# Strassen's product for the input projection of a pooling and memory-attention layer, two blocks of tokens at a time

## The chip, the core and the metric

The kernel runs on one core of a Trainium2 chip. The metric is the device time of one execution in microseconds (us); the kernel before has a median of 645.53 us over three runs (643.67 to 647.44). Work is issued to five engines that run side by side and wait for one another through semaphores: TensorE (PE, matrix products), VectorE (DVE), ScalarE (ACT), GpSimd (POOL) and SyncE (SP, here only an issuer of DMAs). Each engine takes its instructions strictly in order.

## The reference, cut to what matters

With one layer (DEPTH = 1) only the pooling mixer is used. S = 2048 tokens of width 1024, all in float32:

```
hn   = rms_norm(x, norm_g)                          # 2048 x 1024
proj = hn @ pool_w_in                               # 1024 -> 768 | 256 | 1024
u, mq, gate = split(proj)
tok  = ((causal window means of u, widths 2 4 8 16) - u) @ w_group * pool_scale
mem_o = softmax(mq @ mem_k.T / 8) @ mem_v           # 4 heads of 64, 256 memory rows
h    = x + (concat(tok, mem_o) * silu(gate)) @ w_out
out  = rms_norm(h, final_norm_g)
```

`mem_k` and `mem_v` come from the memory `mem` (256 rows) by its own norm and product `w_mem_kv`.

## The kernel before

Every product of float32 matrices is three products in float32r: each operand is split in a rounded part `hi` and a remainder `lo = src - hi` (`_split`, line 43), and `_mm3` (line 54) adds hi*hi, hi*lo and lo*hi. The split costs one cast and one subtraction per operand tile.

At the start the group weights and the scale are folded into the input weights of the mixer (lines 91 to 131: `wus`, the fold, result stored to DRAM as `w_z`). Then four blocks of 512 tokens follow (`block`, line 283). A block has its normalised tokens feature-major in `xh`, `xl` (`prep_block`). Its input projection is sixteen tiles of 128 output columns in the list `order`: two of memory queries ("q"), eight of gate ("g"), six of the pooled mixer ("z"). `project` does one: a 512 KB weight tile is loaded (`load_w`) into the pool `raw` (four buffers), split, and 8 x 3 products of 128 x 128 x 512 are accumulated in one PSUM bank. Scores, transposes and value products of the memory attention are written between the tiles of the same block. The result of every tile stays on chip: the gate in `sg`, the window sums in `win`, the product of both, split, in `bh`, `bl`.

The output projection follows: two halves of 512 columns (`dh`), for each four weight pieces of two 128-row tiles (`w_out[c, dh]`), each 4 token tiles x 2 x 3 products; then residual, sum of squares, last norm, store. The tokens of the next block are loaded and split while it runs (`prep_block` between the two halves; row statistics are gathered earlier by `load_rows` during the input projection).

In block 0 the tokens are not scaled by their row norm ahead of the product: `prep_block(0, None)` uses x * gain alone and the row scale is multiplied into the first results afterwards (`scale`). So the first block's products need neither the row statistics nor the memory.

The order of instructions on each engine is not the order in which they are written: the framework places them by a timeline of its own, except where `keep_in_program_order` or `issue_after` holds them. SP's DMAs of block 0 go in the order written (`_InOrder`).

Of the kernel before, what the change touches and what calls it, by code (L numbers as in the profile page):

```python
# [15 lines left out]
P = 128  # L16
D = 1024
S = 2048
KT = D // P            # 128-row tiles of d_model
BT = 512               # tokens per block  # L20
NB = S // BT
QT = BT // P           # token tiles per block
NMEM = 256
GD = 192               # channels per pooling group
NJ = 6                 # 128-channel tiles of the pooled mixer
WINDOWS = (2, 4, 8, 16)
HALO = 16
EPS = 1e-6


class _InOrder:
    """The queue of SP; until it is free, its transfers go in the order in which they are written down."""

    def __init__(self, tc):
        self.tc = tc
        self.free = False

    def dma_start(self, **kw):
        i = self.tc.nc.sync.dma_start(**kw)  # L39
        return i if self.free else self.tc.keep_in_program_order(i)  # L40


def _split(nc, hi, lo, src, hi_eng):
    """hi = src rounded to float32r, lo = src - hi (exact in float32r)."""
    if hi_eng == "pool":
        nc.gpsimd.tensor_scalar(hi, src, 1.0, 1.0, ALU.mult, ALU.mult)  # L46
    elif hi_eng == "act":
        nc.scalar.copy(hi, src)
    else:
        nc.vector.tensor_copy(hi, src)  # L50
    return nc.vector.tensor_tensor(out=lo, in0=src, in1=hi.bitcast(F32), op=ALU.subtract)  # L51


def _mm3(nc, ps, ahi, alo, bhi, blo, start, stop):
    """ps += a.T @ b from float32r halves of a and b."""
    nc.tensor.matmul(ps, lhsT=ahi, rhs=bhi, start=start, stop=False)  # L56
    nc.tensor.matmul(ps, lhsT=ahi, rhs=blo, start=False, stop=False)  # L57
    nc.tensor.matmul(ps, lhsT=alo, rhs=bhi, start=False, stop=stop)  # L58
# [3 lines left out]
def trunk(ctx, tc, x, xT, mem, memT, norm_g, mem_norm_g, w_mem, w_out, w_in, w_uT, w_g, p_scale, final_g,  # L62
          cinv, out):
    nc = tc.nc
    sp = _InOrder(tc)
    pool = lambda name, bufs, **kw: ctx.enter_context(tc.tile_pool(name=name, bufs=bufs, **kw))
    const = pool("const", 1)
    raw = pool("raw", 4)
    whl = pool("whl", 3)
    big = pool("big", 1)  # L70
    hp = pool("hp", 8)
    zp = pool("zp", 2)
# [8 lines left out]
    # products of zeros bring the tensor engine to its full clock while the first loads are under way  # L81
# [7 lines left out]
    spare = [big.tile([P, KT, BT], F32, name=n).rearrange("p k t -> p (k t)") for n in ("bh", "bl")]  # L89
    wus = [spare[k // 5][:, (k % 5) * 6 * P:(k % 5 + 1) * 6 * P].rearrange("p (g d) -> p g d", g=6) for k in range(KT)]  # L90
    wga = spare[1][:, 18 * P:24 * P].rearrange("p (g e) -> p g e", g=4)
    psc = spare[1][:, 24 * P:30 * P]
    wgb = zp.tile([P, BT], F32, name="rbc", bufs=1)[:, :2 * GD].rearrange("p (a e) -> p a e", a=2)
# [10 lines left out]
    # the last 64 rows of two groups stand on the two halves of the partitions, their columns side by side  # L104
    tails = [whl.tile([P, 2, 2, GD], F32R, name=n) for n in ("whi", "wlo")]
    for t in tails:
        nc.vector.memset(t.bitcast(F32), 0.0)
# [5 lines left out]
    for k in range(KT):  # L113
        zs = wus[k].rearrange("p g d -> p (g d)")
        ut = att.tile([P, 2, 2, P], F32R, name=("qh", "ql", "pth", "ptl")[k % 4], bufs=1)
# [8 lines left out]
        for a, ps in enumerate(pss):  # L124
            c = slice(2 * a * GD, 2 * (a + 1) * GD)
            if k < 6:
                nc.vector.tensor_tensor(out=zs[:, c], in0=ps.rearrange("p l e -> p (l e)"), in1=psc[:, c], op=ALU.mult)
            else:
                nc.scalar.copy(zs[:, c], ps.rearrange("p l e -> p (l e)"))
                nc.gpsimd.tensor_tensor(out=zs[:, c], in0=zs[:, c], in1=psc[:, c], op=ALU.mult)  # L130

# [4 lines left out]
    nc.scalar.dma_start(out=gx, in_=norm_g)  # L136
    half = const.tile([P, QT], F32, name="half")
    nc.vector.memset(half, -0.5)
    halo = const.tile([P, NJ, HALO], F32, name="halo")
    nc.vector.memset(halo, 0.0)  # L140

# [7 lines left out]
    def sum_sq(src, acc):  # L149
        n = src.shape[-1]  # L150
        junk = (small.tile([P, BT], BF16, name="junk", bufs=1)[:, :n] if n <= BT else
                att.tile([P, D], BF16, name="qh", bufs=1))
        nc.scalar.activation(out=junk, in_=src, func=AF.Square, accum_out=acc)  # L153

    def bcast_cols(r, n, dst):
        """dst[:, 128 t + i] = r[i, t] on every partition."""
        ps = ps_mm.tile([P, BT], F32, name="mm")
        for t in range(n):
            rb = small.tile([P, P], F32, name="rb", bufs=4)
            nc.vector.tensor_copy(rb, r[:, t:t + 1].broadcast_to([P, P]))  # L160
            nc.tensor.matmul(ps[:, t * P:(t + 1) * P], lhsT=rb, rhs=ident, start=True, stop=True)
        nc.vector.tensor_copy(dst, ps[:, :n * P])

# [1 line left out]
    # per head the same 64 rows of keys stand on both halves of the partitions  # L165
    khi = const.tile([P, 2, 2, NMEM], F32R, name="khi")
    klo = const.tile([P, 2, 2, NMEM], F32R, name="klo")
    # [tile of keys, pair of heads, head]: the even head's values as [high | low], the odd one's as [low | high]
# [415 lines left out]
```

## Time and profile before

| | us |
|---|---|
| median of three runs | 645.53 |
| span of the profiled execution, first to last instruction | 639.9 |
| PE busy | 613.8 |
| DVE busy | 448.2 |
| POOL busy | 257.5 |
| ACT busy | 236.1 |
| bytes moved by DMA | 93.60 MB |

The page gives the span of the profiled execution; the time of that execution as the runs count it is not listed beside it. The median is 5.6 us above the span, and that difference is used wherever a span is turned into a time. A busy PE is not PE at its peak: products overlap, so that the duration of one (392 ns) is longer than the distance between two.

### The profile page before, as it was taken

To read this page: it belongs to the slowest core of one execution; us is meant where nothing else is said; L and a number is where in the kernel's file an instruction comes from. 1 tells how busy PE (TensorE), PEld (TensorE's weight loads), DVE (VectorE), ACT (ScalarE), POOL (GpSimd) and SP (SyncE) were. 2 spreads that over 40 slices of the span, in tenths; PEclk is the share of its full clock that TensorE was granted. 3 is DMA by queue.
4 is the path that set the end of the run, shared out by engine and by line. 5 is a ranking of instruction groups with operands and counts; after the bars stand their busy time and mean duration, and the time that the engine had idled before them with its cause. 6 is when DMAs were issued, how large, how long until landed. Compare 5 with 4: busy or idle time off the path is not lost.

```text
span 639.9 us, 8205 instructions
## 1 busy us (share of the span) xinstructions
PE 613.8 (96%) x2939; PEld 512.4 (80%) x2939; DVE 448.2 (70%) x673; ACT 236.1 (37%) x503; POOL 257.5 (40%) x211
## 2 busy tenths in 40 slices
PE   7999998999699999999899999999899999999995
PEld 5979786887588888888688888888688888888884
DVE  4875799999938279885847478885846558887235
ACT  2723255533113375522212475522211354532002
POOL 3623384332214155552224155553324254453243
PEclk9999997999999999999999999999899999999998
DMA  8979933413536933232546953232545722132103
GB/s 277 401 232 314 314 139 98 100 66 83 176 128 233 285 44 123 82 99 66 184 145 222 304 43 111 94 99 66 164 135 179 244 69 67 66 99 99 66 1 132
DMA packets 36841, 93.60 MB, mean 146 GB/s; under 512 B 5568, under 2 KB 13120, under 8 KB 36800
## 3 DMA queue, kind: packets, MB, share of 16 engines
q1 hardware_dynamic: 34288, 86.25, 43.9%
q10 hardware_dynamic: 2512, 6.82, 2.9%
q8 instruction: 23, 0.38, 0.2%
q14 instruction: 18, 0.15, 0.1%
HBM read 76.80 MB, written 11.54 MB: 138 GB/s over the span
## 4 chain that ended last, share of the span: by engine, by line
PE 56%; DVE 18%; DMA 10%; issue 5%; POOL 4%; ACT 4%; SPq 1%; ACTq 0%; POOLq 0%; DVEq 0%
PE mm L57 17%; PE mm L58 17%; PE mm L56 17%; DVE wlo L51 5%; DMA raw<-in_xT 3%; POOL win L350 2%; DVE win L364 2%; DMA raw<-w_z 2%; DVE raw L275 2%; PE mm L413 1%; SPq L39 1%; DVE pr L390 1%; DMA h<-in_xT 1%; PE pt L401 1%; DMA raw<-in_w_in 1%
## 5 line engine op out<-in xcount | busy, mean ns | idle before, releaser
L46 POOL TENSOR_SCALAR whi<-raw 128x1024 fp32r<-128x1024 f32 x100 | 127.4, 1274 | 284.8 <-PE mm L57 135.0
L58 PE MATMUL mm<-xh,wlo 128*128 128x512 f32 x512 | 200.7, 392 | 1.7 <-DVE wlo L51 1.7
L56 PE MATMUL mm<-xh,whi 128*128 128x512 f32 x512 | 200.7, 392 | 0.0
L57 PE MATMUL mm<-xl,whi 128*128 128x512 f32 x512 | 200.5, 392 | 0.0
L51 DVE TENSOR_TENSOR wlo<-raw,whi 128x1024 fp32r<-128x1024 f32 x100 | 134.2, 1343 | 57.5 <-POOL whi L46 57.5
L58 PEld LDWEIGHTS mm<-xh,wlo 128*128 128x128 f32 x512 | 96.5, 189 | 22.7 <-DVE wlo L51 2.9
L56 PEld LDWEIGHTS mm<-xh,whi 128*128 128x128 f32 x512 | 96.7, 189 | 18.7
L57 PEld LDWEIGHTS mm<-xl,whi 128*128 128x128 f32 x512 | 96.5, 189 | 18.6 <-DVE xl L272 0.3
L57 PE MATMUL mm<-wlo,bh 128*128 128x512 f32 x248 | 98.2, 396 | 5.7 <-DVE wlo L51 5.7
L56 PE MATMUL mm<-whi,bh 128*128 128x512 f32 x248 | 95.0, 394 | 4.9 <-DVE h L515 4.9
L58 PE MATMUL mm<-whi,bl 128*128 128x512 f32 x248 | 97.1, 394 | 0.0
L350 POOL TENSOR_TENSOR win<-win 128x525 f32<-128x525 f32 (+4 forms) x40 | 62.7, 1567 | 3.1
L153 ACT ACTIVATE junk<-h 128x512 bf16<-128x512 f32 (+1 forms) x33 | 20.4, 618 | 116.9 <-DVE h L515 116.8
L57 PEld LDWEIGHTS mm<-wlo,bh 128*128 128x128 f32 x248 | 47.4, 191 | 16.7 <-DVE wlo L51 6.9
L56 PEld LDWEIGHTS mm<-whi,bh 128*128 128x128 f32 x248 | 47.2, 190 | 15.5 <-issue 5.3
L58 PEld LDWEIGHTS mm<-whi,bl 128*128 128x128 f32 x248 | 47.3, 191 | 9.8
L350 POOL TENSOR_TENSOR win<-z 128x527 f32<-128x527 f32 x24 | 29.6, 1235 | 25.2 <-DVE z L337 10.7
L385 ACT ACTIVATE pr<-sc,nm 128x256 f32<-128x256 f32 x64 | 29.7, 470 | 18.4 <-DVE nm L381 18.2
L390 DVE TENSOR_SCALAR pr<-pr,rc 128x256 f32<-128x256 f32 x64 | 34.3, 577 | 0.9
L364 DVE SCALAR_TENSOR_TENSOR win<-win,z 128x512 f32<-128x512 f32 (+1 forms) x32 | 30.4, 949 | 4.2 <-POOL win L350 3.7
L515 DVE TENSOR_TENSOR h<-mm,h 128x512 f32<-128x512 f32 x31 | 21.1, 686 | 16.8 <-PE mm L58 16.7
L335 ACT COPY z<-halo 128x16 f32<-128x16 f32 x24 | 4.8, 203 | 73.9 <-DVE win L364 53.0
(157 smaller groups left out, 771.8 us busy)
## 6 DMA issues: line engine op xcount, KB each, us to landing
raw<-in_w_in SPq DMA_DIRECT2D x40, 512.0 KB, 4.5
raw<-in_w_out SPq DMA_DIRECT2D x32, 512.0 KB, 3.4
raw<-w_z SPq DMA_DIRECT2D x24, 512.0 KB, 4.6
h<-in_x SPq DMA_DIRECT2D x16, 512.0 KB, 6.8
raw<-in_xT SPq DMA_DIRECT2D x12, 512.0 KB, 4.1
out_y<-h ACTq DMA_DIRECT2D x12, 512.0 KB, 2.9
mq<-win SPq DMA_DIRECT2D x32, 128.0 KB, 6.0
h<-in_xT SPq DMA_DIRECT2D x4, 512.0 KB, 8.9
```

Source lines behind the costliest of these rows:

```text
L46: nc.gpsimd.tensor_scalar(hi, src, 1.0, 1.0, ALU.mult, ALU.mult)
L51: return nc.vector.tensor_tensor(out=lo, in0=src, in1=hi.bitcast(F32), op=ALU.subtract)
L56: nc.tensor.matmul(ps, lhsT=ahi, rhs=bhi, start=start, stop=False)
L57: nc.tensor.matmul(ps, lhsT=ahi, rhs=blo, start=False, stop=False)
L58: nc.tensor.matmul(ps, lhsT=alo, rhs=bhi, start=False, stop=stop)
L153: nc.scalar.activation(out=junk, in_=src, func=AF.Square, accum_out=acc)
L275: nc.vector.scalar_tensor_tensor(out=xk, in0=xk, scalar=g, in1=rb, op0=ALU.mult, op1=ALU.mult)
L350: nc.gpsimd.tensor_tensor(out=cur[rows, a:], in0=prev[rows, a:], in1=prev[rows, off:N - step], op=ALU.add)
L364: nc.vector.scalar_tensor_tensor(out=yt[rr], in0=sums[g][rr, HALO:], scalar=1.0 / WINDOWS[g], in1=z[rr, HALO:], op0=ALU.mult, op1=ALU.subt ...
L385: nc.scalar.activation(out=pr[:, h, :], in_=ps[:, h, :], func=AF.Exp, bias=nm[:, h:h + 1], accum_out=su[:, h:h + 1])
L390: nc.vector.tensor_scalar_mul(pr[:, h, :], pr[:, h, :], rc[:, h:h + 1])
L515: added = nc.vector.tensor_tensor(out=h, in0=ps, in1=h, op=ALU.add)
```

## The change

The input projection is done for two blocks (1024 tokens) and two column tiles at a time, by Strassen's product in the form with seven products (Winograd's): the depth of 1024 is cut in two halves, the two blocks are the two columns of B, the two weight tiles the two rows of A. `group` forms four sums of weight quarters on POOL and makes seven products of depth 512 (4 x 3 matmuls each); `x_forms` makes the seven token operands, which fill fourteen slots. Query, gate and pooled results go through DRAM (`q_d`, `g_d`, `y_d`) and are read back for the attention and for `branch` in the output projection; half of the second pair's token operands go through DRAM too (`xs_d`). The attention of both blocks is written between the products. The scale of the rows is in the tokens from the start. Pools: `raw` has three buffers instead of four, and carries rows, tokens, weights and branch tiles alike; the row tiles kept in `hp` and the double weight tiles in `whl` are gone.

```diff
@@ token operands @@
+    def x_forms(s, k, rbs, X, later):
+        r = []
+        for kk in (k, k + KH):
+            rt = raw_tile((P, 2, BT))
+            sp.dma_start(out=rt, in_=xT[2 * s:2 * s + 2, :, kk, :].rearrange("b p t -> p b t"))
+            for a in range(2):
+                nc.vector.scalar_tensor_tensor(out=rt[:, a, :], in0=rt[:, a, :], scalar=gx[:, kk:kk + 1], in1=rbs[a], ...)
+            r.append(rt)
+        b11, b12, b21, b22 = r[0][:, 0, :], r[0][:, 1, :], r[1][:, 0, :], r[1][:, 1, :]
+        t1, t2, t4 = (st.tile([P, BT], F32, name="s") for _ in range(3))
+        forms = {1: b11, 2: b21, 3: b22, 4: t4, 5: t1, 6: t2, 7: b12}
+        sub(g, t1, b12, b11)
+        sub(g, t2, b22, t1)
+        sub(g, b12, b22, b12)
+        sub(g, t4, b21, t2)
+        for p in (1, 6, 2, 5, 7, 3, 4):
+            if p in X:
+                _split(nc, X[p][0][:, k, :], X[p][1][:, k, :], forms[p], "act")
+        for i, p in enumerate(later):
+            nc.gpsimd.dma_start(out=xs_d[i, k], in_=forms[p])
@@ seven products for two column tiles @@
+    def group(s, X, w1, w2, take, between):
+        r1, r2 = raw_tile((P, KT, P)), raw_tile((P, KT, P))
+        sp.dma_start(out=r1, in_=w1)
+        sp.dma_start(out=r2, in_=w2)
+        a11, a12, a21, a22 = r1[:, :KH], r1[:, KH:], r2[:, :KH], r2[:, KH:]
+        add(g, s1, a21, a22)
+        sub(g, s2, s1, a11)
+        sub(g, a21, a11, a21)
+        sub(g, s4, a12, s2)
+        def product(p, onto=None):
+            hi, lo = chunk(forms[p], "act", (P, KH, P), "pool" if p in (2, 5, 3) else "dve")
+            ps = bank[p] = bank[onto] if onto else ps_mm.tile([P, BT], F32, name="mm")
+            for k in range(KH):
+                _mm3(nc, ps, hi[:, k, :], lo[:, k, :], X[p][0][:, k, :], X[p][1][:, k, :], ...)
+            between()
+            return ps
...
@@ output projection: operands read back @@
+    def branch(b, e, bh, bl):
+        rt = raw_tile((P, 2, BT))
+        sp.dma_start(out=rt[:, 0, :], in_=y_d[b][e])
+        sp.dma_start(out=rt[:, 1, :], in_=g_d[b][e])
+        nc.vector.tensor_tensor(out=rt[:, 0, :], in0=rt[:, 0, :], in1=rt[:, 1, :], op=ALU.mult)
+        _split(nc, bh[e // KH][:, e % KH, :], bl[e // KH][:, e % KH, :], rt[:, 0, :], "act")
...
-            for group in ((3,), (2,), (1, 0)):
-                ws = {c: load_w(w_out[c, dh], [P, 2, BT]) for c in group}
+            for ic, c in enumerate(order):
+                if dh == 0:
+                    for e in (2 * c, 2 * c + 1):
+                        branch(b, e, bh, bl)
+                wr = raw_tile((P, 2, BT))
+                sp.dma_start(out=wr, in_=w_out[c, dh])
+                ws = [chunk(wr[:, kk, :], "pool") for kk in range(2)]
+                between()
...
@@ the order of the whole @@
+    memory()
+    rbs = row_scales(0, row_stats(0))
+    for k in range(KH):
+        x_forms(0, k, rbs, X, ())
+    project_in(0, X, scales)          # scales: row statistics of blocks 2 and 3, between groups 7 and 8
+    project_out(0, (5, 7), ORDER, gf, some)   # some: x_forms(1, k) per weight piece
+    project_out(1, (3, 4), ORDER, gf, some)   # some: operands 5 and 7 read back
+    project_in(1, X, lambda: None)
+    project_out(2, (5, 7), ORDER, gf, lambda: None)
+    project_out(3, (3, 4), ORDER, gf, lambda: None)
```

PE's queue before, from the last products of the fold (`ptl` and `bl` hold input weights, `whi` group weights) to the first products of the input projection (`xh`, `xl`: tokens of block 0):

```order
L121 MATMUL mm<-bl 128x192 x2
L56 MATMUL mm<-whi,ptl 128x384
L57 MATMUL mm<-wlo,ptl 128x384
L58 MATMUL mm<-whi,ptl 128x384
L56 MATMUL mm<-xh,whi 128x512
L57 MATMUL mm<-xl,whi 128x512
L58 MATMUL mm<-xh,wlo 128x512
```

PE's queue of the change where its first product of the input projection stands (`x5h` and `wh` above it are the memory and its weights, `rb` the row statistics of the memory and of both blocks, `x1h` the token operand of product 1):

```order
L53 MATMUL sc<-x5h,wl 128x256 x2
L52 MATMUL pt<-wl,x5h 128x256
L53 MATMUL pt<-wh,x5l 128x256
L171 MATMUL mm<-ident,rb 128x128 x10
L51 MATMUL mm<-x1h,wh 128x512
L52 MATMUL mm<-x1l,wh 128x512
L53 MATMUL mm<-x1h,wl 128x512
```

The first products of the input projection have moved from behind the fold to behind the memory's products and the row statistics of two blocks.

SP's queue before, from the loads of the fold to the products of the memory (`h` is the pool `hp`):

```order
L39 DMA bl<-in_w_uT 128x768 x3
L39 DMA raw<-in_w_in 128x1024
L39 DMA h<-in_xT 128x1024 x4
L39 DMA raw<-in_w_in 128x1024 x2
L39 DMA h<-in_x 128x1024 x4
L39 DMA raw<-in_w_in 128x1024
L39 DMA gm<-in_mem_norm_g 128x8
L39 DMA raw<-in_memT 128x1024 x2
L39 DMA raw<-in_w_mem 128x1024 x2
```

The same queue of the change, from the memory's weights to the first weight tiles of the input projection:

```order
L196 DMA raw<-in_w_mem 128x1024 x2
L583 DMA w_z<-x4l 128x6x128 x2
L162 DMA raw<-in_mem 128x1024 x2
L162 DMA raw<-in_x 128x1024 x8
L272 DMA raw<-in_xT 128x2x512 x8
L306 DMA raw<-in_w_in 128x1024
L307 DMA raw<-in_w_in 128x1024
```

Rows, tokens and the first weight tiles now go one behind the other through the three buffers of `raw`, where before the tokens came first and had buffers of their own.

SP's queue before in the output projection of block 1 (blocks 2 and 3 alike):

```order
L39 DMA raw_2709<-in_w_out 128x1024
L39 DMA raw_2739<-in_w_out 128x1024
L39 DMA raw_2769<-in_w_out 128x1024
L39 DMA raw_2775<-in_w_out 128x1024
L39 DMA raw_2831<-in_xT 128x1024
L39 DMA raw_2839<-in_xT 128x1024
```

The same queue of the change in the first half of the output projection of block 0, one weight piece and the start of the next (`y_d0` and `g_d0` are the results read back):

```order
L500 DMA raw_2681<-y_d0_287 128x512
L501 DMA raw_2681<-g_d0_291 128x512
L553 DMA raw_2687<-in_w_out 128x1024
L272 DMA raw_2697<-in_xT 128x2x512
L272 DMA raw_2701<-in_xT 128x2x512
L500 DMA raw_2746<-y_d0_287 128x512
L501 DMA raw_2746<-g_d0_291 128x512
L500 DMA raw_2752<-y_d0_287 128x512
L501 DMA raw_2752<-g_d0_291 128x512
L553 DMA raw_2758<-in_w_out 128x1024
```

Each weight piece of this half now stands with two branch tiles and two token tiles in the same three buffers.

## Rows read from the trace of the kernel before

**Rows 1.** The page's head and first part: span; busy time, share and instructions by engine.

```profile
span 639.9 us, 8205 instructions
PE 613.8 (96%) x2939; PEld 512.4 (80%) x2939; DVE 448.2 (70%) x673; ACT 236.1 (37%) x503; POOL 257.5 (40%) x211
```

**Rows 2.** Busy time by stretch: start:end, length, engines' busy us, granted clock, DMA.

```profile
280.00:320.00 40.00, 37.79 (x171) 31.14 (x170) 30.57 (x39) 9.49 (x20) 14.29 (x9) 1.00 0.40 127
320.00:440.00 120.00, 120.00 (x576) 100.37 (x575) 82.40 (x123) 50.35 (x109) 52.09 (x42) 1.00 0.50 140
440.00:480.00 40.00, 37.14 (x157) 30.26 (x156) 25.53 (x34) 8.95 (x19) 10.19 (x7) 0.96 0.43 133
```

**Rows 3.** Timeline of PE: start us, us, instruction; 27 products lie from one start to the next.

```profile
26.59 0.39 PE L56 MATMUL mm<-xh,whi 128*128 128x512 f32 x1
...
198.73 0.39 PE L56 MATMUL mm<-xh,whi 128*128 128x512 f32 x1
...
204.85 0.39 PE L56 MATMUL mm<-xh,whi 128*128 128x512 f32 x1
```

**Rows 4.** Groups of instructions by line, PE, first 110 us: count, busy us, mean ns.

```profile
L56 PE MATMUL mm<-xh,whi 128*128 128x512 f32 x84 | 33.7, 401 | 0.0
...
L58 PE MATMUL mm<-xh,wlo 128*128 128x512 f32 x83 | 33.3, 401 | 1.7 <-DVE wlo L51 1.7
```

**Rows 5.** DMA issues of the whole span: KB each, median us from issue to landing.

```profile
raw<-in_w_out SPq DMA_DIRECT2D x32, 512.0 KB, 3.4
h<-in_x SPq DMA_DIRECT2D x16, 512.0 KB, 6.8
raw<-in_xT SPq DMA_DIRECT2D x12, 512.0 KB, 4.1
```

**Rows 6.** Groups of instructions by line, whole span, shapes apart: count, busy us, mean ns.

```profile
L350 POOL TENSOR_TENSOR win<-z 128x527 f32<-128x527 f32 x24 | 29.6, 1235 | 25.2 <-DVE z L337 10.7 <-ACT z L339 6.5 <-ACT bh L48 6.1
L153 ACT ACTIVATE qh<-h 128x1024 bf16<-128x1024 f32 x16 | 16.9, 1056 | 20.3 <-DMA h<-in_x 20.0
L275 DVE SCALAR_TENSOR_TENSOR raw<-raw,gx,rbc 128x512 f32<-128x512 f32 x24 | 17.5, 778 | 17.5 <-DMA raw<-in_xT 13.7 <-issue 3.8
L51 DVE TENSOR_TENSOR xl<-raw,xh 128x512 fp32r<-128x512 f32 x24 | 16.7, 749 | 0.0
L48 ACT CAST xh<-raw 128x512 fp32r<-128x512 f32 x24 | 14.7, 620 | 27.9 <-DVE raw L275 27.5
```

**Rows 7.** The chain that ended last, at a block's change: start us, us, what.

```profile
291.55 4.08 DMA raw<-in_xT
295.89 0.54 issue
...
306.57 4.14 DMA raw<-in_xT
```

**Rows 8.** Who waited for whom: us in total, times, longest us.

```profile
ACT vhl L48 <- DMA klo<-klo: 9.8, 1, 9.8
```

**Rows 9.** Timeline of POOL and of DVE in block 0.

```profile
78.22 1.92 POOL L350 TENSOR_TENSOR win<-z 128x527 f32<-128x527 f32 x1 [1.93 <-issue]
84.78 1.07 POOL L350 TENSOR_TENSOR win<-z 128x527 f32<-128x527 f32 x1
...
78.01 1.21 DVE L51 TENSOR_TENSOR wlo<-raw,whi 128x1024 fp32r<-128x1024 f32 x1
86.33 2.08 DVE L51 TENSOR_TENSOR wlo<-raw,whi 128x1024 fp32r<-128x1024 f32 x1
```

**Rows 10.** Timeline of PE where it waited in the first output projection.

```profile
175.36 0.77 PE L56 MATMUL mm<-whi,bh 128*128 128x512 f32 x1 [4.93 <-DVE h L515]
175.93 0.63 PE L57 MATMUL mm<-wlo,bh 128*128 128x512 f32 x1
176.35 0.63 PE L58 MATMUL mm<-whi,bl 128*128 128x512 f32 x1
```

**Rows 11.** Granted clock by stretch, PE alone: busy us, clock, DMA share, GB/s.

```profile
175.00:177.00 2.00, 1.64 (x4) 0.53 0.91 246
```

## What is predicted, before the change was run

> **What bounds the kernel now.** I read the page's first part, then the busy time by stretch, then PE's timeline, and last the chain where a block changes. PE is busy 613.8 of 639.9 us [rows 1]. That figure counts overlapping products, so the stretches decide: from 320 to 440 us PE has no idle time at all [rows 2]. There the distance between two products of 512 columns counts, not their duration: 27 of them start within 204.85 - 198.73 = 6.12 us, 0.227 us each [rows 3]. The kernel is bound by the number of products, apart from its start and some 10 us of waits after it: 2.2 us from 280 to 320, 2.9 from 440 to 480 [rows 2] and 4.9 at 170 to 175 [rows 10]. Between blocks the work on the next tokens is a chain of loads through `raw`, three of them issued 15 us from the first to the last [rows 7], and PE hardly feels it, because the output projection runs meanwhile on operands that are on chip.
>
> The start matters as much here. The first product of the input projection stands at 26.59 us, right behind the fold [rows 3], since tokens of block 0 need neither row statistics nor memory. By 110 us 251 of its 1536 products are done (84, 84 and 83 in three lines, the middle one not shown) [rows 4].
>
> **What goes.** Eight groups per pair of blocks, seven products of 12 matmuls, two pairs: 1344 for 1536, so 192 x 0.227 = 43.6 us of PE. All else on PE stays in count. The scales multiplied into first results in block 0 go, and some DVE work moves to ACT; neither engine is the bound, so this is worth nothing.
>
> **What the start costs.** Now the memory, all statistics of two blocks and all token operands come ahead of the first product, in that order on SP's queue and through three buffers.
> - The fold ends at 26.6 as before. The last memory weights leave `raw` about 6.5 us later (a load of 4.1 [rows 5], cast and subtraction of two halves, some 2.4): 33.
> - Two tiles of memory rows and eight of x: each a load of 4.5 (4.1 to 6.8 [rows 5]), 0.5 of issue [rows 7], a Square of 1.06 [rows 6], three at a time: 10/3 x 6.06 = 20, 53. ACT stood 9.8 us behind the copies of the keys before [rows 8]; in the new order the last four Squares stand behind the same DMAs. I take half, 5: 58.
> - Row scale (one POOL step, small DVE steps, a product): 4, an estimate from the POOL and DVE rows [rows 6]: 62.
> - First of four `x_forms`: two scalings at 0.78, three POOL steps at 1.24, cast 0.62, subtraction 0.75 [rows 6]: 6.6, 69. Each further one can load its second tile only when the one ahead has split operand 7: load 4.1, issue 0.5, two scalings, two POOL steps, cast, subtraction: 10.0, three times: 99.
> - Product 6 of the first group waits for the second weight tile, which takes the buffer freed last: 4.1 + 0.5 + two POOL sums + split = 8.5: 107. Product 1 (2.7 us) has run by then, so the dense part starts as if at 105.
> - POOL and DVE block each other: a remainder takes 2.08 us instead of 1.21 and a window step 1.92 instead of 1.07 when the other runs [rows 9]. One such 0.9 us in each of four `x_forms`: 4. I take 108.
>
> Ends: 93 with loads of 3.4 and neither stall; 132 with loads of 6.8 and the whole 9.8.
>
> The Trainium skill ("SBUF — State Buffer", Who interferes with whom) says why: an instruction of DVE with two inputs in SBUF and one of POOL that reads SBUF hold a shared port in turn. The trace agrees in the two pairs named. By that rule alone an `x_forms` is serial on both engines, 4 x 1.24 + 4 x 0.78 + 7 x 0.75 = 13.3 us, not 10.0; the start would be 114 and the sum below 723.
>
> **What the rest costs.** Before, 639.9 - 110 = 529.9 us follow the first 110, with 1285 input products; the change has 1344 to do, 59 more: 13.4. Its own waits, 10.0, go with the code that made them: 533. (A little attention that stood before 110 us is left to the range.) To this come waits at places that the change makes:
> - A. Rows of blocks 2 and 3 run through `raw` between groups 7 and 8: eight tiles, two buffers, 4.1 + 0.5 + 1.06 each = 23, then the group's own tile 6, against 84 x 0.227 = 19 of products in group 7: 10 (0 to 20).
> - B. First half of the output projection of block 0. A weight piece is 24 products, 5.4 us, and needs two branch tiles, one weight tile and, in the same queue, two token tiles. In the order shown the token tiles hold two buffers until POOL has formed and stored the operands, and the third serves the rest in turn: branch tile 4.1 + 0.5 + product 0.75 + cast 0.62 + subtraction 0.75 = 6.7, twice, weights 3.4 + 0.5 + 1.4 = 5.3; 18.7 a piece against 5.4. The first is preloaded, three are not: 40. The cover was the output products themselves, and they are too few. Ends: DVE's own steps (4 x 0.78 and 9 x 0.75, 9.8 a piece): 13; one more branch tile that waits: 60.
> - C. Block 1, first half: four tiles read back for operands 5 and 7; five tiles in three buffers, 5 x 6.7 / 3 = 11.2 for 5.4 in two pieces, 12 less what is loaded ahead: 8 (0 to 12).
> - D. Return to the input projection: operand 3 needs slot 3, which the output projection reads to its end, and its tiles keep the buffers that the second weight tile needs: 2.1 + 4.6 + 2.5 + 1.4 less product 1: 8 (3 to 12).
> - E. After the wait of 4.9 us the granted clock was 0.53 [rows 11], the level of 1.2 GHz, and products stood 0.42 apart [rows 10], for seven of them: 1.4 a restart. Three that no other wait hides: 4 (0 to 8).
>
> Sum: 108 + 533 + 10 + 40 + 8 + 8 + 4 = 711 of span; the median stands 5.6 above the span [rows 1], so 717. Break-even lies where start and A to E together are 645.5 - 5.6 - 533 = 107; the saving of 43.6 is in the 533 already.
>
> **Rivals.**
> - Faster: the loads run at 3.4 us, ACT does not stall, and the scheduler's order keeps branch tiles ahead of token tiles, so that only D is left: 93 + 533 + 8 + 5.6 = 640. For it: 32 weight loads had a median of 3.4 [rows 5], and between blocks PE lost only 2 to 3 us [rows 2]. Against it: there the tokens were not in the queue of the operands that PE waited for. It decides from start plus waits under 104.
> - Only the start and A: the output projection finds its tiles loaded. 108 + 533 + 10 + 5.6 = 657. For it: outside the start DMA uses at most half of its time [rows 2]. Against it: three buffers, not bandwidth.
> - The groups themselves become bound by POOL: four sums, three remainders, on average four window steps; at the blocked 1.92 [rows 9] 21 us, with the copies of edges 23, against 19 of products: 16 x 4 = 64 more, 781. Against it: at 1.24 they are 13.6.
>
> **Chances.** Forecast (680 to 760) 0.55; start and A alone 0.19; POOL-bound groups 0.16; faster or even 0.10. Half a per cent (3 us) is about what these runs can tell from no change. Faster by more than that needs both halves of the first rival: 0.06; within it 0.05; slower 0.89. Range 655 to 785: it takes in the start-only case and the POOL-bound one, and leaves out the faster one.
>
> **What would show it.** After: the first product with `x1h` between 90 and 125 us, with PE idle for tens of us before; in the first half of the output projection of block 0 four bursts of 24 products with waits of 10 to 15 us on `raw` tiles or branch splits between them; one wait of about 10 us near the last group of the first input projection; in the groups PE busy over 95%. Wrong if the first product stands before 90, if the output projection of block 0 takes under 55 us, or if PE's idle time is spread evenly through the groups (then POOL or ACT is the bound).

## The result, and the profile after

The kernel after has a median of 780.81 us (779.15 to 787.02, four runs); the kernel before, on the same chip, 645.31. The ratio is 1.213, 95% interval 1.207 to 1.219: slower, 64 us above the 717 that were forecast. The profiled execution has a span of 777.6 us.

The first lines of its page, answering to [rows 1]:

```profile
span 777.6 us, 8816 instructions
...
PE 607.0 (78%) x2755; PEld 496.8 (64%) x2755; DVE 473.6 (61%) x713; ACT 341.9 (44%) x683; POOL 386.2 (50%) x381
...
PE   8921049999999868343695695999999999899695
```

PE is busy for nearly as long as before (607.0 against 613.8 us), though the change does 192 products of the input projection fewer. In the 40 slices there are two large holes, at the start and in the middle, and a small one near the end. DMA moves 131.66 MB instead of 93.60, because results and some of the token operands now go through DRAM. Busy time by stretch, answering to [rows 2] (columns: stretch, its length, then busy us with count for PE, PEld, DVE, ACT, POOL, then granted clock, DMA share, GB/s):

```profile
40.00:103.00 63.00, 5.40 (x20) 4.23 (x20) 45.71 (x69) 26.75 (x52) 24.76 (x17) 0.53 0.44 141
200.00:240.00 40.00, 39.90 (x209) 33.73 (x208) 23.74 (x39) 31.86 (x65) 28.70 (x28) 1.00 0.31 106
...
312.00:385.00 73.00, 29.66 (x98) 22.65 (x96) 50.12 (x49) 11.90 (x20) 39.83 (x40) 0.69 0.52 178
385.00:478.00 93.00, 71.00 (x288) 56.81 (x288) 57.77 (x99) 25.35 (x57) 22.21 (x29) 0.89 0.63 220
```

In the groups (200 to 240) PE does not wait, as in [rows 2]. Beside the output projections of blocks 0 and 1 (312 to 478) DVE is busier than PE at first, and the granted clock falls to 0.69. PE's timeline where it waited longest, answering to [rows 3, 10] (in brackets the idle time ahead and who ended it):

```profile
103.13 0.79 PE L51 MATMUL mm<-x1h,wh 128*128 128x512 f32 x1 [39.35 <-ACT wh L38]
113.50 0.80 PE L51 MATMUL mm<-x6h,wh 128*128 128x512 f32 x1 [4.96 <-ACT wh L38]
...
331.08 2.08 PE L51 MATMUL mm<-wh,x7h 128*128 128x512 f32 x4 [13.49 <-POOL wh L36]
351.11 2.07 PE L51 MATMUL mm<-wh,x5h 128*128 128x512 f32 x4 [11.57 <-POOL wh L36]
368.74 2.07 PE L51 MATMUL mm<-wh,x5h 128*128 128x512 f32 x4 [10.52 <-POOL wh L36]
384.93 0.77 PE L51 MATMUL mm<-wh,x7h 128*128 128x512 f32 x1 [7.76 <-DVE mq L566]
```

The pieces of block 0 follow each other at 16 to 20 us, and four products take 2.07 us there, 0.43 from one to the next: the lower of the two clock levels, 1.2 GHz [rows 10, 11]. To place the whole difference I split both spans in four: up to the first dense product (of `x6h` after, the first of the input projection before); idle gaps of PE behind it; what the records at half clock lost (taken as half of PE's busy time in the stretches granted 1.2 GHz); and the rest, products at full clock.

| span, us | before | after |
|---|---|---|
| first dense product | 26.6 | 113.5 |
| gaps of PE behind it | 15.4 | 95.1 |
| lost at 1.2 GHz | 6.2 | 28.8 |
| the rest | 591.7 | 540.2 |
| span | 639.9 | 777.6 |

So the saving is there: the rest is 51.5 us shorter, 43.6 of it the products that are gone; the other 7.9 I put down to products of the memory and of the first group, which now stand ahead of the 113.5. The start took 86.9, the gaps 79.7 and the clock 22.6.

### The profile page after: what moved, and what is told of

Read it like the earlier page. It is cut to its first block, busy times and chain, and to the rows that moved or that the text cites. A ratio compares the mean times of both kernels' runs of the same rounds, so it can differ in the third digit from the quotient of the medians.

```text
span 777.6 us, 8816 instructions
## 1 busy us (share of the span) xinstructions
PE 607.0 (78%) x2755; PEld 496.8 (64%) x2755; DVE 473.6 (61%) x713; ACT 341.9 (44%) x683; POOL 386.2 (50%) x381
## 2 busy tenths in 40 slices
DMA packets 61695, 131.66 MB, mean 169 GB/s; under 512 B 7632, under 2 KB 17232, under 8 KB 61648
## 4 chain that ended last, share of the span: by engine, by line
PE 30%; DMA 24%; DVE 19%; ACT 10%; POOL 8%; issue 7%; SPq 1%; ACTq 0%; POOLq 0%; DVEq 0%
PE mm L51 9%; PE mm L52 9%; PE mm L53 8%; DMA raw<-in_w_out 7%; DVE wl L46 3%; DMA raw<-in_x 3%; DMA raw<-g_d 3%; DMA raw<-in_xT 3%; DVE raw L274 2%; POOL s L86 2%; POOL wh L36 2%; DMA raw<-xs_d 2%; DVE win L385 2%; ACT L442 1%; DMA raw<-in_w_in 1%
## 5 line engine op out<-in xcount | busy, mean ns | idle before, releaser
L46 DVE TENSOR_TENSOR wl<-raw,wh 128x512 fp32r<-128x512 f32 x120 | 109.3, 925 | 83.5 <-ACT wh L38 42.0
L36 POOL TENSOR_SCALAR wh<-raw 128x512 fp32r<-128x512 f32 x72 | 51.3, 723 | 148.5 <-DMA raw<-in_w_out 97.5
L375 POOL TENSOR_TENSOR win<-win 128x527 f32<-128x527 f32 (+2 forms) x64 | 77.1, 1207 | 3.5 <-DVE win L89 1.4
L46 POOL TENSOR_TENSOR wl<-s,wh 128x512 fp32r<-128x512 f32 x32 | 43.5, 1360 | 32.0 <-ACT wh L38 23.8
L38 ACT CAST wh<-raw 128x512 fp32r<-128x512 f32 x64 | 39.8, 621 | 43.4 <-PE mm L52 32.9
L86 POOL TENSOR_TENSOR s<-raw,s 128x512 f32<-128x512 f32 x32 | 47.7, 1490 | 14.0 <-DVE raw L274 13.3
L51 PEld LDWEIGHTS mm<-x1h,wh 128*128 128x128 f32 x64 | 13.2, 206 | 56.2 <-ACT wh L38 54.0
L38 ACT CAST wh<-s 128x512 fp32r<-128x512 f32 x48 | 29.7, 620 | 38.5 <-PE mm L52 20.0
L502 DVE TENSOR_TENSOR raw<-raw 128x512 f32<-128x512 f32 x32 | 24.1, 753 | 36.8 <-DMA raw<-g_d 36.8
L385 DVE SCALAR_TENSOR_TENSOR win<-win 64x512 f32<-64x512 f32 (+1 forms) x32 | 33.9, 1061 | 7.1 <-POOL win L375 6.6
L86 POOL TENSOR_TENSOR raw<-raw 128x512 f32<-128x512 f32 x24 | 36.3, 1513 | 0.0
L51 PE MATMUL mm<-wh,x3h 128*128 128x512 f32 x60 | 23.7, 439 | 12.7 <-POOL wh L36 12.7
L86 POOL TENSOR_TENSOR s<-raw 128x512 f32<-128x512 f32 x8 | 15.3, 1910 | 33.9 <-DVE raw L274 18.5
L89 POOL TENSOR_TENSOR s<-raw 128x512 f32<-128x512 f32 x16 | 21.1, 1319 | 21.9 <-DMA raw<-in_w_in 17.4
```

Of the source, the lines that this page charges most:

```text
L36: return nc.gpsimd.tensor_scalar(hi, src, 1.0, 1.0, ALU.mult, ALU.mult)
L38: return nc.scalar.copy(hi, src)
L46: return e.tensor_tensor(out=lo, in0=src, in1=hi.bitcast(F32), op=ALU.subtract)
L86: return eng.tensor_tensor(out=o, in0=a, in1=b, op=ALU.subtract)
L375: nc.gpsimd.tensor_tensor(out=cur[rows, o:], in0=prev[rows, o:], in1=prev[rows, off:N - step], op=ALU.add)
L385: nc.vector.scalar_tensor_tensor(out=yt[rr], in0=sums[g][rr, HALO:], scalar=1.0 / WINDOWS[g], in1=z[rr, HALO:], op0=ALU.mult, op1=ALU.subt ...
```

## The experiments

All ratios are against the kernel before on the same chip, measured beside each run; "dense" is the first product with `x6h`; the last two columns are gaps of PE over 1 us in the output projections of blocks 0 and 1.

| run | us | ratio, 95% | dense | block 0 | block 1 |
|---|---|---|---|---|---|
| the change | 780.8 | 1.213 (1.207 to 1.219) | 113.5 | 43.3 | 14.7 |
| e1 own tiles | 762.9 | 1.186 (1.180 to 1.192) | 115.2 | 24.1 | 12.1 |
| e2 no forms | 727.9 | 1.131 (1.125 to 1.137) | 113.6 | 3.9 | 13.4 |
| e3 filled | 777.8 | 1.209 (1.203 to 1.214) | 113.0 | filled | filled |
| e4 late scale | 766.3 | 1.192 (1.186 to 1.198) | 99.3 | 42.5 | 13.2 |
| e5 start tiles | 772.6 | 1.203 (1.196 to 1.210) | 108.8 | 40.9 | 15.4 |
| e6 spread | 761.4 | 1.185 (1.179 to 1.190) | 113.1 | 24.7 | 16.2 |
| e7 together | 744.1 | 1.156 (1.151 to 1.162) | 103.0 | 25.1 | 9.7 |
| e8 sums on DVE | 758.3 | 1.176 (1.169 to 1.183) | 105.9 | 34.8 | 14.6 |
| e9 all | 714.1 | 1.109 (1.100 to 1.117) | 88.6 | 16.5 | 10.0 |
| e10 branch | 783.7 | 1.213 (1.206 to 1.220) | 113.1 | 51.7 | 7.8 |
| e11 all, branch | 704.6 | 1.091 (1.083 to 1.099) | 89.9 | 19.8 | 0 |
| e12 all, weight sums on DVE | 715.8 | 1.107 (1.101 to 1.114) | 87.8 | 19.0 | 0 |

**e1, the buffers in block 0.**

```diff
+own = slot(3 + k // 2, "hl"[k % 2], (P, 2, 2, BT), F32) if s else None
-    rt = raw_tile((P, 2, BT))
+    rt = own[:, kk // KH] if s else raw_tile((P, 2, BT))
```

> Second pair's token tiles no longer pass through the three raw buffers: in the output projection of block 0 they are loaded into the operand places 3 and 4, which are free there, and the operands read back (5, 7, 3, 4) are loaded into their low half and split in place. Theory (three shared buffers are what the first half of the output projection of block 0 waits for): its three waits of 13.5, 11.6 and 10.5 us before a piece fall to 3 to 6 each, what DVE's own steps leave; the two of block 1 (8.0 and 6.7) and the one at the return (7.3) fall to 3 or less; with fewer slow-clock stretches the time is 730 to 755 instead of 781. Rival (POOL and DVE, which hold each other up, are what the pieces wait for, buffers or not): the three waits stay above 9 each, the time above 768.

Between the two: the waits of the first half fell from 35.6 to 22.2 us (9 to 18 by the theory, over 27 by the rival), and block 1 hardly moved. What is left has two causes in the rows. The largest wait, 7.67 us, ends with POOL's cast, which had waited for its weight tile while the DMA engines were busy all the time (the stretch's last columns: DMA share 1.02, 377 GB/s); the waits of 3.75, 3.86 and 1.83 us end with DVE. PE's gaps, POOL's row and the stretch, then DVE's rows:

```profile
334.60 2.08 PE L51 MATMUL mm<-wh,x5h 128*128 128x512 f32 x4 [7.67 <-POOL wh L36]
340.43 0.80 PE L52 MATMUL mm<-wl,x5h 128*128 128x512 f32 x1 [3.75 <-DVE wl L46]
...
333.70 1.86 POOL L36 TENSOR_SCALAR wh<-raw 128x512 fp32r<-128x512 f32 x2 [12.17 <-DMA raw<-in_w_out]
...
325.00:334.00 9.00, 1.93 (x9) 1.27 (x7) 4.72 (x8) 3.04 (x5) 0.30 (x1) 0.85 1.02 377
...
337.89 0.68 DVE L46 TENSOR_TENSOR x2l<-x3h,x2h 128x512 fp32r<-128x512 f32 x1
338.49 0.68 DVE L46 TENSOR_TENSOR x1l<-x3l,x1h 128x512 fp32r<-128x512 f32 x1
339.09 0.68 DVE L46 TENSOR_TENSOR x2l<-x3l,x2h 128x512 fp32r<-128x512 f32 x1
339.69 0.68 DVE L46 TENSOR_TENSOR wl<-raw,wh 128x512 fp32r<-128x512 f32 x1
```

That weight tile landed 8.16 us after its issue at 325.37, where the one of the same piece in the change took 5.45: with the buffers free, the loads come all at once and each is later. Behind it, the split of the weight (`wl`) that PE waits for stands behind a row of operand splits that nobody needs yet.

**e2, the forming left out.**

```diff
-X = x_slots((1, 6, 2))
-for k in range(KH):
-    work.append(lambda k=k: x_forms(1, k, rbs, X, (5, 7, 3, 4)))
+X = {p: X[p] for p in (1, 6, 2)}
```

> Leaves out the forming of the second pair's operands 1, 6 and 2 (it uses the first pair's) and reads token tiles where it read 5, 7, 3 and 4 back. Everything else of the two output projections stays. Theory (the forming beside the output projection of block 0 is what costs there): the three waits of 35.6 us in all and the one of 7.8 behind them fall to under 12 together, the half-clock stretches after them (about 9 us lost) mostly go, time 725 to 742. Rival (a piece's own branch tiles and weights are too slow through three buffers, as the two waits of block 1 without any forming suggest): 20 us or more of waits stay in block 0, time above 750.

The theory held: 3.9 of 43.3 us are left in block 0, 8.8 us less are lost to the clock, and 52.9 us of time go. So nearly all of block 0's waiting is the forming beside it, with its loads and stores, which go too. Block 1 keeps its 13.4: those waits are another matter.

**e3, the clock.**

```diff
+i = tc.keep_in_program_order(nc.tensor.matmul(pt, lhsT=f[:, :P], rhs=f[:, :BT], start=True, stop=True))
```

> Adds products whose results nobody reads (40, 40, 36 and 24 of 128x512) in the waits of the output projection of block 0 and 24 each in two waits of block 1, so that PE is busy in them. Theory (about 30 us of the missing time is not waiting but products at 1.2 GHz after each wait): the bursts after the filled waits run at a granted clock of 1.0 and start 0.23 us apart, the waits themselves stay where they were, and 10 to 15 us go: 765 to 772. Rival (the bursts are spaced by their operands, not by the clock, or the filling products delay the real ones): 779 or more.

My theory was not met: the time lies between its range and the rival's, and the interval overlaps that of the change. Of the three bursts only the second runs at full clock, four products in 1.20 us; all three start where they started before:

```profile
331.18 2.07 PE L51 MATMUL mm<-wh,x7h 128*128 128x512 f32 x4 [9.83 <-POOL wh L36]
350.81 1.20 PE L51 MATMUL mm<-wh,x5h 128*128 128x512 f32 x4 [2.45 <-POOL wh L36]
368.82 2.08 PE L51 MATMUL mm<-wh,x5h 128*128 128x512 f32 x4 [3.90 <-POOL wh L36]
```

331.18, 350.81 and 368.82 against 331.08, 351.11 and 368.74. The pieces are paced by the work that feeds them: after the one burst that ran faster, the next came no earlier. The lost time at 1.2 GHz fell from 28.8 to 20.4 us, and no gain can be told from the times. Where products follow densely it may be worth something: in this trace block 1's two late pieces start 2 us earlier than in the change (420.38 and 434.61 against 422.51 and 436.50). The half-clock stretches ahead of a dense run (after the start, at the return) were not tried alone.

**e4, the scale of the rows after the product.**

```diff
-nc.vector.scalar_tensor_tensor(out=rt[:, a, :], in0=rt[:, a, :], scalar=gx[:, kk:kk + 1], in1=rbs[a], ...
+nc.scalar.mul(rt, rt, gx[:, kk:kk + 1])
...
+nc.vector.tensor_tensor(out=o, in0=ps, in1=RB[a], op=ALU.mult)      # in scaled(), for each result
```

> Operands are formed from unscaled tokens (gain alone, on ACT); the scale of the rows is multiplied into each result, 64 more multiplies on DVE. The rows of blocks 0 and 1 load into attention tiles; those of blocks 2 and 3 one by one from the second group on. (win has 6 buffers and u 2 to make room for the two scales.) Theory (the start is one chain, memory - rows - scale - four operand formings - second weight tile, and 22 us of it are the rows): dense products start at 85 to 92 instead of 113.5, and the waits of 6.0 and 3.4 near the last group of the first input projection go: time 735 to 755. Rivals: the forming itself sets the start and only 3 to 8 us go there (770 or more); or the 64 multiplies of 0.69 make DVE the bound in the groups, PE busy there under 95%, and what the start gains is lost (775 or more).

The start came 14 us earlier (first product 89.45 instead of 103.13), less than the theory's 21 to 28. The waits of 6.0 and 3.4 near the last group went, but one of 4.8 came in the attention. The second rival took part of it back: in the groups PE is now idle where it was not (a stretch of this run, columns as above):

```profile
200.00:240.00 40.00, 37.13 (x184) 30.43 (x182) 27.60 (x43) 33.09 (x64) 25.88 (x23) 0.96 0.37 126
```

37.1 of 40 us against 39.9. 14.5 us were won of the 26 to 46 expected; the time lies between the theory's range and both rivals'. Block 0 kept 42.5 us of waits, though the four scalings of each forming had left DVE.

**e5 and e8, what a forming costs at the start.** In e5 the tiles of the second and fourth forming go into idle attention tiles; in e8 one word changes:

```diff
+rt = (raw_tile((P, 2, BT)) if s or k % 2 == 0 else att.tile([P, 2, BT], F32, name=n, ...))     # e5
...
-        g = nc.gpsimd
+        g = nc.vector                                                                      # e8
```

> At the start the token tiles of the second and fourth forming go into four attention tiles, which are idle there, instead of the three raw buffers. Theory (each further forming is late by a load that cannot start before the one ahead has given its buffers back, 4.6 us three times, and the second weight tile likewise): the formings follow each other at about 8 us instead of 11.5, the dense products start at 95 to 102 instead of 113.5, time 763 to 771. Rival (POOL and DVE hold each other up, four sums of 1.7 us and seven remainders in turn, and that sets the 11.5): start at 109 or later, time above 776.

> The four sums of each forming of token operands run on DVE instead of POOL, nothing else. Theory (POOL and DVE take turns: a sum of 1.27 us alone takes 1.7 beside remainders and holds each of them from 0.68 to 1.75, so a forming is the sum of both engines' steps, 4 x 1.27 + 11 x 0.62 = 11.9 us; on DVE alone 15 x 0.62 = 9.3): the formings of the start get 8 to 10 us shorter in all and the dense products start at 103 to 106 instead of 113.5; the waits of block 0's output projection shrink by some 8; time 762 to 771. Rival (the two engines work side by side, and DVE, already the busier, gets 4 x 0.68 us more in each forming): dense start at 116 or later, time 784 or more.

With four more tiles the dense products start 4.7 us earlier, not 12 or more, about where e5's rival had them; the time, 772.6, lies between the two ranges. The 4.7 is a net figure. In e5 the rows' loads went later (the first of x at 41.16 instead of 36.41), and the second of the two row scales was ready 5 us later. The two ends of the formings, the last copy of a scale and the last remainder, first in the change and then in e5:

```profile
64.72 0.68 DVE L172 COPY sg<-mm 128x512 f32<-128x512 f32 x1
107.82 0.68 DVE L46 TENSOR_TENSOR x4l<-s,x4h 128x512 fp32r<-128x512 f32 x1
```

```profile
69.72 0.69 DVE L172 COPY sg<-mm 128x512 f32<-128x512 f32 x1
106.89 1.75 DVE L46 TENSOR_TENSOR x4l<-s,x4h 128x512 fp32r<-128x512 f32 x1
```

From the one to the other it takes 43.1 us in the change, 38.2 in e5 and 36.8 in e8 (64.80 to 101.56). The wait for the second weight tile behind it, 5.0 us in the change, is 0.1 in e5 and 4.4 in e8. So buffers and turns both cost at the start, and which costs more these runs do not show.

With the sums on DVE the dense products start 7.6 us earlier and the time falls by 22 us: e8's theory, better than its range. The reason is what [rows 9] showed in small: in the change itself POOL and DVE start a step each every 1.67 us, in turns. Its DVE and its POOL rows, and then DVE's of e8, where it works alone:

```profile
70.59 1.74 DVE L46 TENSOR_TENSOR x5l<-s,x5h 128x512 fp32r<-128x512 f32 x1
72.26 1.75 DVE L46 TENSOR_TENSOR x6l<-s,x6h 128x512 fp32r<-128x512 f32 x1
...
70.08 1.70 POOL L86 TENSOR_TENSOR raw<-raw 128x512 f32<-128x512 f32 x1
71.75 1.70 POOL L86 TENSOR_TENSOR s<-raw,s 128x512 f32<-128x512 f32 x1
```

```profile
69.10 0.68 DVE L86 TENSOR_TENSOR raw<-raw 128x512 f32<-128x512 f32 x1
69.71 0.68 DVE L46 TENSOR_TENSOR x5l<-s,x5h 128x512 fp32r<-128x512 f32 x1
70.31 0.68 DVE L86 TENSOR_TENSOR s<-raw,s 128x512 f32<-128x512 f32 x1
70.91 0.68 DVE L46 TENSOR_TENSOR x6l<-s,x6h 128x512 fp32r<-128x512 f32 x1
```

A sum and a remainder take 1.67 us on two engines and 1.2 on one. Block 0's gaps fall by 8.5 us by the same edit.

**e6, the formings in other places** (on top of e1).

```diff
-if work:
+turn[0] += 1
+if turn[0] in (2, 5, 6, 7, 13, 14):
     work.pop(0)()
```

> The kernel with own token tiles, and besides the four formings stand at pieces 2, 5, 6 and 7 of the output projection of block 0 instead of 1 to 4, and the two operands read back at pieces 5 and 6 of block 1 instead of 1 and 2, so that they lie beside the second halves, which load no branch tiles. Theory (with own tiles what is left is DVE's order: formings queued ahead of the split of the weights that PE waits for): the waits of 24 us in block 0 fall under 10 and the two of 7.0 and 5.2 in block 1 under 4 each; 738 to 750 instead of 763. Rival (DVE has 108 us of work in the two projections, which hold 87 us of products, so the waits only move): the sum of the waits in the two blocks stays above 25, time above 756.

The rival's numbers came: the gaps only moved (40.9 us in the two blocks, 36.2 in e1). Its reason is not shown. In the two output projections of the change DVE is busy 107.9 us (50.12 + 57.77 above) beside 384 x 0.227 = 87 of products, but this counts the time for which POOL holds it up: in e8, with sixteen sums more, DVE is busy 100.6 us there (301 to 458). One other order was tried, and it did not help.

**e7 and e9, the terms together.** e7 joins e1, e4, e5 and e6; e9 adds to it

```diff
-        g = nc.gpsimd
+        g = nc.vector
...
-ws = [chunk(wr[:, kk, :], "pool") for kk in range(2)]
+ws = [chunk(wr[:, kk, :], "act") for kk in range(2)]
```

and the rows ahead of the token tiles.

> All four changes together: late scale of the rows, own token tiles, spread formings, and the start's tiles in the attention's. If the terms add up as the single runs showed them (start 113.5 to about 82, waits of block 0 from 43 to about 10 since the scaling of the tokens has left DVE, block 1 to about 6) the time is 715 to 735. If DVE is the bound of the two output projections, or of the groups through the 64 multiplies, it stays above 740. In both cases it stays above the kernel before, since the start alone is some 55 us later than there against 43.6 saved.

> The kernel with all four changes together, and besides the sums of the formings on DVE, all rows of blocks 0 and 1 loaded ahead of the token tiles that use the same attention tiles (there PE's copies of the scale waited for the last rows until 98 us), and the output weights cast on ACT instead of POOL. Theory of turns: dense start at 75 to 82, block 0's waits under 15, time 712 to 726. Rival (DVE's own work is the bound in the formings and in both output projections, and the sums add to it): dense start above 90, time above 738. In both cases slower than the kernel before: a start 50 us later than there, against 43.6 saved.

e7 missed its theory's range and lies in the rival's, above 740. One cause that is not the rival's stands on PE: copies of the row scale, for which the last rows came late, stood ahead of ready products.

```profile
98.10 0.77 PE L172 MATMUL mm<-ident,rb 128*128 128x128 f32 x2 [36.81 <-DVE rb L171]
```

e9 came to 714.1, inside the range of the theory of turns. Two of its terms were missed: block 0 kept 16.5 us (under 15 expected), and the dense start at 88.6 is later than the 75 to 82 expected. DVE is busy 33.6 of the 34 us from 51 to 85 there, and the second weight tile was issued only at 79.47; that DVE is the cause is not shown by a run of its own.

**e10, e11, e12, the branch tiles.** e10 on the change, e11 on e9; e12 has `g = nc.vector` in `group` too.

```diff
-rt = raw_tile((P, 2, BT))
-sp.dma_start(out=rt[:, 0, :], in_=y_d[b][e])
-sp.dma_start(out=rt[:, 1, :], in_=g_d[b][e])
+h, l = bh[e // KH][:, e % KH, :], bl[e // KH][:, e % KH, :]
+sp.dma_start(out=l.bitcast(F32), in_=y_d[b][e])
+sp.dma_start(out=h.bitcast(F32), in_=g_d[b][e])
```

> Branch tiles of the four output projections no longer pass through the raw buffers: they load into the operand places themselves (y into the low half, the gate into the high half), the product goes through a win buffer, which is idle there. Theory (two branch tiles and one weight tile a piece in three shared buffers are what block 1, and blocks 2 and 3, wait for): the waits of 8.0 and 6.7 in block 1 fall under 3 each, the 9.4 of blocks 2 and 3 under 4 in all, those of block 0 from 43 to 20 to 28, as with own token tiles; time 748 to 762 instead of 781. Rival (DVE's queue, where the last sums of the block ahead and the splits of operands stand in front of the split of the weights): block 1 keeps more than 10, blocks 2 and 3 more than 7, time above 768.

> The kernel of 714 us (late scale, own tiles, spread formings with their sums on DVE, output weights cast on ACT) with the branch tiles in place as well. Theory of the buffers: its waits of 26 us in the four output projections halve, 696 to 705. Rival (DVE): 709 or more.

> As the run before, and the four sums of weights in each of the 16 groups on DVE instead of POOL. Theory of turns (a sum holds the port twice as long on POOL, 1.27 against 0.62 us): the some 20 us of short waits inside the two input projections shrink, 4 to 9 us faster than the run before. Rival (DVE, at two thirds busy in the groups, becomes the one that is late): 2 us or more slower than the run before. In either case not below the kernel before.

e10's theory fell: no change in time. Block 1 got better (7.8 for 14.7), but block 0 worse, with one gap of 25.83 us. SP's rows show it (SPq is its DMA queue):

```profile
316.26 0.32 SPq L500 DMA_DIRECT2D x4l<-y_d  x1
...
328.73 0.38 SPq L272 DMA_DIRECT2D raw<-in_xT  x1
329.39 0.32 SPq L259 DMA_DIRECT2D sg<-row  x1
330.03 0.32 SPq L501 DMA_DIRECT2D x5h<-g_d  x1
343.01 0.38 SPq L272 DMA_DIRECT2D raw<-in_xT  x1
347.63 0.33 SPq L554 DMA_DIRECT2D raw<-in_w_out  x1
```

and PE's answer to it:

```profile
355.42 2.08 PE L51 MATMUL mm<-wh,x5h 128*128 128x512 f32 x4 [25.83 <-POOL wh L36]
```

Since branch tiles now have places of their own, all of them, block 1's too (into `x4l`, `x3l`), were issued early. The queue goes in order, token tiles took the buffers that this freed, and the third weight tile of block 0 was issued only at 347.63, behind a token tile before which the queue had stood for 12.7 us. Where the forming was short already (e11) the same edit gave 9.5 us (704.6, the end of its theory's range); but the gaps did not halve: block 1's 10.0 went, one of 16.2 is left in block 0, and 11.0 us of waits stand in block 2. The 16.2 ends with an operand (`x5h`) whose gate tile was issued at 310.13 and took 14.1 us to land, while the DMA engines were busy all the time (share 1.00), among others with tiles of the next blocks. The stretch, and the tile among the DMA issues from 300 to 325 us:

```profile
305.00:325.00 20.00, 5.18 (x23) 3.94 (x21) 14.33 (x23) 13.23 (x19) 5.05 (x10) 0.73 1.00 366
...
x5h<-g_d SPq DMA_DIRECT2D x1, 256.0 KB, 14.1
```

In e12 the weights' sums on DVE cost 11 us, on its rival's side: against e11's trace the gaps are 4.7 us longer, the half-clock stretches lose 8.2 more, and the start is 2.1 earlier; why, the runs do not show. e11 is the best of these kernels and still 9.1% slower than the kernel before (8.3 to 9.9); its dense start is at 89.9, 63 us later than before, against 43.6 saved. No run put the first groups ahead of the memory, as the kernel before has it, and none kept the results on chip; what these two cost is not shown.

## Why the prediction was right, and where it was short

The direction and its two reasons held: the operands of the first group come late, and the forming of the next ones does not fit beside an output projection (e2). The size was short, and that the time lies in the stated range at all is luck: 780.8 is outside the forecast's own 680 to 760, and the range reaches to 785 only to take in the POOL-bound groups, which did not happen. In span, 66.6 us are missing:

| term | forecast | measured |
|---|---|---|
| start | 108 | 113.5 |
| rest | 533 | 547.1 |
| A, rows between groups 7 and 8 | 10 | 8.8 |
| the last group | - | 3.4 |
| B, block 0, first half | 40 | 35.6 |
| block 0, into the second half | - | 7.8 |
| C, block 1 | 8 | 14.7 |
| D, return | 8 | 8.4 |
| blocks 2 and 3 | - | 9.5 |
| E, clock | 4 | 28.8 |
| sum | 711 | 777.6 |

- **Start.** Rows ended at 58.6 (58 forecast). The miss came next: the row scales were ready at 65.4 (62) and the first forming ended at 76.3 (69). The other three ended 11.9, 11.5 and 8.9 us one after the other, 32 in all against 30 forecast. The forecast priced them as loads that wait for a buffer, with 0.9 us for the port; e5 and e8 show that both cost, and that the port was put too low. The rule of the Trainium skill ("SBUF — State Buffer", Who interferes with whom) gave 114 for the start, near the 113.5 measured, but by 13.3 us for each of these three formings; so e8 and the rows in turns bear out that the engines hold each other up, and not the rule's sum.
- **Rest.** 14 too low. 7.0 of it are waits in no other row, all of 1.5 us or less. The forecast let "a little attention" that stood before 110 us go to the range; it was 28 products of 128x256 and 12 of 128x128, for which PE was busy 7.3 us.
- **A, B, D** held within 5 us. In B three bursts with waits of 10.5 to 13.5 came as described, at 16 to 20 us (18.7 forecast). Of the cause, three buffers, e1 shows under half, so part of the agreement is luck. In what e1 leaves, DMA at its limit and DVE's order both appear; no run took one of them away alone. The forecast set "three buffers, not bandwidth" against its second rival: once the buffers are free, in e1 and e11, the DMA engines are busy all the time ahead of the waits.
- **Not priced.** DVE also writes out the first half's sums, and stood behind formings when PE wanted the banks (7.8). Blocks 2 and 3 have four waits of 1.2 to 4.7 us for the cast of a weight tile, though nothing of a next block is formed beside them. Ahead of the longest, at 738 us, the DMA engines were busy all the time (729 to 738 us, share 1.03); otherwise their cause stays open.
- **C** was forecast at about half the measured size. Neither own tiles (12.1) nor leaving out the forming (13.4) moved it much; branch tiles out of `raw` halved it (7.8), so the buffers that branch and weight tiles share are a part. In e1 the DMA engines are busy 0.96 to 0.98 of the time ahead of its two waits (395 to 405 and 411 to 419 us), so bandwidth may be another; that is not shown alone.
- **E.** The worst miss in size: the forecast counted three restarts at 1.4 us; there were thirteen stretches at 1.2 GHz with products in them, at 1.5 to 3.1 us each. Yet in e3 a burst at full clock between block 0's waits did not bring the next one forward. For such paced stretches B and E should have been one term: their period.
- **Rivals.** 781 was the number of the POOL-bound groups, but not by that way: in the groups PE is busy 99.8% at 200 to 240 us. That DMA uses at most half of its time outside the start, said for the second rival, is a mean of long stretches: the page of the kernel before has two of its 16 us slices at 0.9 (208 to 224 and 352 to 368 us).
- **The 5.6 us** between span and time, added to every sum, is no cost within an execution: the change's profiled one has a span of 777.6 and a time of 779.34, 1.7 more.

## What to carry to other kernels

Ask of a product with fewer multiplications first what must be ready before its first product, and who forms it: here what stands ahead of it put the first dense product 87 us later, at 113.5 instead of 26.6, twice what the saved products give back. When sums and remainders of whole tiles alternate between POOL and DVE, price them as turns and try them on one engine; but try it per place, since the same move won 22 us in the formings (e8) and lost 11 in the groups (e12). Work moved beside a short stage has to fit each engine's time there and the DMA engines', not only PE's. When waits are paced by feeding, a faster clock need not help, and freer buffers help only in part (18 us in e1, nothing in e10): a freed buffer lets an in-order queue put something else first, and more loads at once make each one later.

## What was not expected of the hardware

- Two engines in turns were slower than one: 1.67 us for a sum on POOL and a remainder on DVE side by side, 1.2 us for both on DVE. Alone a POOL sum of 128x512 takes 1.26 to 1.27 us (the change, 110.19 to 112.75 us).
- A burst at half clock between waits that are paced by others need not cost time: with filling products ahead of it one of three bursts ran at full clock (four products in 1.20 us instead of 2.07), and all three starts stayed within 0.3 us.
- Freed buffers made loads slower: with the DMA engines busy all the time, a weight tile of 512 KB took 8.16 us to land (e1) and a gate tile of 256 KB 14.1 us (e11); the medians in the change are 4.3 and 4.0.
